# SBUF laid out so that every tile read by TensorE begins at a multiple of 512 bytes, with the kernel's small tiles together at the beginning

## The chip, the core and the metric

The kernel runs on one core of one Trainium2 chip. The metric is the device time of one execution in microseconds (us); three executions of the kernel before took 1311.05, 1311.29 and 1311.66 us, so the median is 1311.29 us.

## The reference, cut to what matters

The program is a two-layer decoder trunk over one sequence of 512 tokens, 1024 wide, in float32. In short form:

```python
h = x
h = h + rglru_mixer(rmsnorm(h), ...)   # layer 0: w_in 1024 x 2560, conv, gates, scan, w_out 1280 x 1024
h = h + conv_ffn(rmsnorm(h), ...)      # w_in 1024 x 6144, conv of width 3, gelu(a) * b, w_out 3072 x 1024
h = h + nsa_mixer(rmsnorm(h), ...)     # layer 1: q, k, v; compressed, selected and window attention, gates, w_out
h = h + conv_ffn(rmsnorm(h), ...)
return rmsnorm(h)
```

Nearly all of the arithmetic is in the weight matrices: two feed-forward blocks, the recurrent block's projections and the attention block's projections. The result has to be close to float32.

## The kernel before, in words

**Products.** Activations are kept transposed: a tile of 128 features (partitions) by 512 tokens. Every float32 operand is split into a high part that TensorE's one-pass float32 form holds exactly (`hi`) and the rest (`lo`), and a product is three matmuls, `hi*hi`, `hi*lo` and `lo*hi`, accumulated in one PSUM bank. This is `mm3` (lines 211 to 217): line 213 multiplies the weights' high part with the activations' high part, line 214 the same weights with the activations' low part, line 215 the weights' low part with the activations' high part. The weights are the stationary operand (128 x 128, that is 512 bytes of each partition), the activations the moving operand (128 x 512, 2048 bytes of each partition).

**Weights.** A weight tile is 128 x 1024 (4096 bytes of each partition), eight stationary operands. `_dma` loads it as `wraw` through SP's queue, `_split` makes `whi` on ScalarE (line 184) and `wlo` on VectorE or GpSimd (line 185). `wtile` (line 151) gives two weight tiles of three a buffer in the pool `wp` (named `wraw`, `whi`, `wlo`) and every third one a buffer in the pool `wx` (named `wrawx`, `whix`, `wlox`); during the attention block `wx` is closed and all tiles come from `wp`.

**Activations.** The normalised inputs of a block are `xh0` to `xh7` and `xl0` to `xl7`; the hidden values of a feed-forward block are `fh0` to `fh23` and `fl0` to `fl23` (`ffn`, from line 630); those of the recurrent block `hh`, `hl`, its gates' inputs `ch`, `cl` with weights `ghi`, `glo`; the attention block has keys `K2h`, `K2l`, queries `qa`, `qb`, values `V2`, probabilities `P`, `ph`, `sq`, outputs `oh`, `ol` (for two of the four groups these reuse the names `K2h`, `K2l`).

**Order of the work.** The four blocks follow one another: recurrent, feed-forward, attention, feed-forward. In the first, second and fourth the order of the instructions is the program's; in the attention block every step has a due time (`FILL`, `WIN`, `LAT_S`, `LAT_V` and so on), and the steps are issued sorted by it (`at` and `perform`), each engine in that order. In that block projections and output products stand between the attention's own matmuls.

**Where tiles lie.** The places in SBUF follow from the program alone: pools stand one behind another, tiles in a pool stand in the order in which their names first appear, and each is rounded up to 32 bytes of a partition. The program's own scratch and constants take the first 16,512 bytes, which is 128 more than a multiple of 512. Counted modulo 512, the kernel before places things so. First come `prm` (1520 bytes, rounded to 1536) and `cst` (3176, rounded to 3200), so `x0` to `x7` begin at 256. `mhalf` and `warm` take 64 bytes, so `xh`, `xl` and the pool `wp` (`wraw`, `whi`, `wlo`) begin at 320, and so do `ssum` and `sq`. `nv` and `rtok` (64 bytes) put `rbc` at 384, and the two `fv` and two `frt` (128 bytes) bring the next pool to 0: `wx` (`wrawx`, `whix`, `wlox`), and behind it `fh` and `fl`, or the attention's `K2h`, `K2l`, `V2`. In the recurrent block nine tiles of 64 bytes and `sp` (96) stand before `hh` and `hl`, which begin at 160, as do `ghi`, `glo`, `ch` and `cl`. In the attention block `gtok` (768 bytes) puts `qa` and `qb` at 256, the eight tiles `sm`, `nm`, `c` (256 bytes) put `P` at 0, `mx` (64) puts `ph` at 64, and `smc` (64) puts `ch`, `cl`, `oh`, `ol` at 128.

Of the kernel before, what the change touches and what calls it, by code (L numbers as in the profile page):

```python
# [10 lines left out]
F32 = mybir.dt.float32  # L11
F32R = mybir.dt.float32r
AF = mybir.ActivationFunctionType
# [6 lines left out]
NB = 10  # L20
# [51 lines left out]
P_CW, P_CB, P_GB, P_AP = 40, 80, 90, 110  # L72
P_FW, P_FB = 120, 264
P_B1, P_POS = 312, 316
P_END = 380

C_ID, C_D, C_DC, C_SC, C_ROW, C_ONE, C_SL = 0, 128, 640, 768, 776, 777, 778
C_END = 794
# [22 lines left out]
class Trunk:  # L101
# [166 lines left out]
    def norm_finish(self, newps):  # L268
        T, V = self.T, self.V
        ps = newps()  # L270
        for t in range(4):
            T.matmul(ps[:, t:t + 1], self.ssum[:, 128 * t:128 * t + 128], self.cst[:, C_ONE:C_ONE + 1],
                     start=True, stop=True)
        v = self.np_.tile([128, 4], F32, name="nv", bufs=1)
        V.tensor_scalar(v, ps[:, :4], 1.0 / 1024.0, 1e-6, op0=ALU.mult, op1=ALU.add)
        self.rtok = self.np_.tile([128, 4], F32, name="rtok", bufs=1)
        self.G.tensor_tensor(self.rtok, v, self.mhalf, op=ALU.pow)

    def norm_spread(self, newps):
# [5 lines left out]
        self.rbc = self.np_.tile([128, NT], F32, name="rbc", bufs=1)  # L285
        self.S.activation(self.rbc, ps, AF.Copy)


    def start(self):
        nc, a = self.nc, self.a  # L290
        self.prm = self.cp.tile([128, P_END], F32, name="prm")
        self.cst = self.cp.tile([128, C_END], F32, name="cst")
        self.x = [self.cp.tile([128, NT], F32, name=f"x{k}") for k in range(KD)]
        self.plan()
        self.tins, self.tgrp, self.manual = [], None, False
        self.mhalf = self.cp.tile([128, 4], F32, name="mhalf")
        self.V.memset(self.mhalf, -0.5)
        warm = self.cp.tile([128, 4], F32, name="warm")
        self.S.activation(warm, self.mhalf, AF.Copy)
        self._dma(0)  # L300
        self._dma(1)
        self.wd = 2
        nc.scalar.dma_start(self.prm[:, :P_CW], a["prm"][:, :P_CW])
        self._half(0, 0, True)
        for k in range(KD):
            nc.sync.dma_start(self.x[k], a["x"][k])
            if k in START:
                self._half(*START[k], True)
        self._dma(2)
        self.wd = 3  # L310
        nc.sync.dma_start(self.cst, a["cst"])
        nc.sync.dma_start(self.prm[:, P_CW:], a["prm"][:, P_CW:])
        self.ident = self.cst[:, C_ID:C_ID + 128]

    def warm_up(self, n):
# [53 lines left out]
    def final(self, ts, newps, sq=None):  # L369


        T, V, prm = self.T, self.V, self.prm
        n = (ts.stop - ts.start) // 128
        parts = [self.ssum[:, ts]] + ([sq] if sq is not None else [])
        ps = newps()
        for t in range(n):
            for j, p in enumerate(parts):
                T.matmul(ps[:, t:t + 1], p[:, 128 * t:128 * t + 128], self.cst[:, C_ONE:C_ONE + 1],
                         start=(j == 0), stop=(j == len(parts) - 1))
        v = self.np_.tile([128, 4], F32, name="fv")  # L380
        V.tensor_scalar(v[:, :n], ps[:, :n], 1.0 / 1024.0, 1e-6, op0=ALU.mult, op1=ALU.add)
        rt = self.np_.tile([128, 4], F32, name="frt")
        self.G.tensor_tensor(rt[:, :n], v[:, :n], self.mhalf[:, :n], op=ALU.pow)
        yield
        ps = newps()
# [219 lines left out]
    def softplus(self, hp):  # L605
        V, S = self.V, self.S
        t = lambda nm: hp.tile([128, NB], F32, name="sp_" + nm)
# [13 lines left out]
            V.tensor_scalar(po, po, 2.0 / k, None, op0=ALU.add)  # L621
        V.tensor_mul(po, po, q)
        V.tensor_add(po, po, mx)
        sp = hp.tile([128, 2, NB], F32, name="sp")
        V.tensor_scalar(sp[:, 0], po, 4.0, None, op0=ALU.mult)
        V.tensor_scalar(sp[:, 1], po, -8.0, None, op0=ALU.mult)
        return sp
# [72 lines left out]
    def nsa(self):  # L700
        S, V, G, T, prm, cst = self.S, self.V, self.G, self.T, self.prm, self.cst
        tc, a = self.tc, self.a
        with ExitStack() as s:
# [6 lines left out]

            Vc = kp.tile([128, 4, 4, 128], F32R, name="Vc")
            G.memset(Vc.bitcast(F32), 0.0)
            gtok = kp.tile([128, 4, 48], F32, name="gtok")
            Q = {}

            def project():
# [182 lines left out]
                S.activation(Vc[rs, i, :, :64], pkv[rs], AF.Copy)  # L899
                V.tensor_sub(Vc[rs, i, :, 64:], pkv[rs], Vc[rs, i, :, :64].bitcast(F32))  # L900

            junk = self.np_.tile([128, 4], F32, name="nv", bufs=1)
            self.tact(junk, self.mhalf, AF.Exp)
            q_tile(1)
            cs.close()
# [19 lines left out]
            def compressed(g, s0, d, newps=None):  # L925
# [25 lines left out]
                    V.tensor_add(v4(st["X"]), v4(st["pc"]), dt.unsqueeze(2).to_broadcast([128, 4, 4, 32]))  # L951

                def mx():
                    st["mx"] = ap_.tile([128, 16], F32, name="mx", bufs=1)
                    V.reduce_max(st["mx"], v3(st["X"]), axis=AX.X)

                def sub():
# [5 lines left out]
                        self.G.tensor_mul(v4(st["X"])[:, i], v4(st["X"])[:, i], sl)  # L963

                def norm():
                    sm = st["sm"] = ap_.tile([128, 4, 4], F32, name="smc", bufs=1)
                    V.reduce_sum(sm.rearrange("p i r -> p (i r)"), v3(st["X"]), axis=AX.X)
                    V.reciprocal(sm, sm)
                    V.tensor_mul(sm, sm, gtok[:, :, 4 * g:4 * g + 4])
# [38 lines left out]
            def scores(g, i, brs, steps):  # L1008
# [20 lines left out]

                def red(b):  # L1030
                    if b == 0:
                        st["sm"] = ap_.tile([128, 2, 4], F32, name="sm", bufs=3)
                        st["nm"] = ap_.tile([128, 2, 4], F32, name="nm")
                        st["c"] = ap_.tile([128, 2, 4], F32, name="c", bufs=3)
                    pt = newP(F32)
                    for r in range(b * per, b * per + per):
                        for br in brs:
                            sl = cols(r, br)
                            Ps[g, i, br].append(pt[:, sl])
                            V.tensor_tensor_reduce(pt[:, sl], st["sp", b][:, sl],  # L1040
                                                   cst[:, C_D + 384 - 128 * i:C_D + 512], -SLOPE[4 * g + r],
                                                   3e38, ALU.add, ALU.min, accum_out=st["nm"][:, br, r:r + 1])
# [246 lines left out]
```

## Time and profile before

| | |
|---|---|
| median of three executions | 1311.29 us |
| the profiled execution | 1311.32 us |
| its span, first to last instruction | 1309.5 us |
| granted TensorE clock, mean of the span | 0.996 |
| PE busy (matmul) | 1295.0 us, 99% |
| PE weight loads | 1062.5 us, 81% |
| VectorE, ScalarE, GpSimd busy | 787.2, 612.8, 242.2 us |
| matmuls | 6158 |

A matmul's recorded end is modelled and lies past the start of the next one, so a matmul of 512 columns is shown with about 390 ns while the next one starts about 227 ns after it. How long a matmul holds the engine is therefore read from starts: the start of one row of the timeline, the start of a later one, and the count of matmuls between. Where two groups of the same shape have different means, the difference of the means is the difference of the distances between starts.

### The profile page before, as it was taken

To read this page: it belongs to the slowest core of one execution; us is meant where nothing else is said; L and a number is where in the kernel's file an instruction comes from. 1 tells how busy PE (TensorE), PEld (TensorE's weight loads), DVE (VectorE), ACT (ScalarE), POOL (GpSimd) and SP (SyncE) were. 2 spreads that over 40 slices of the span, in tenths; PEclk is the share of its full clock that TensorE was granted. 3 is DMA by queue.
4 is the path that set the end of the run, shared out by engine and by line. 5 is a ranking of instruction groups with operands and counts; after the bars stand their busy time and mean duration, and the time that the engine had idled before them with its cause. 6 is when DMAs were issued, how large, how long until landed. Compare 5 with 4: busy or idle time off the path is not lost.

```text
span 1309.5 us, 16269 instructions
## 1 busy us (share of the span) xinstructions
PE 1295.0 (99%) x6158; PEld 1062.5 (81%) x6158; DVE 787.2 (60%) x1270; ACT 612.8 (47%) x983; POOL 242.2 (18%) x254
## 2 busy tenths in 40 slices
PE   9999999999999999999999999999999999999996
PEld 7888888888888888888787778888888888888886
DVE  7899875555555533327557978875655555542222
ACT  6788743333333322222458878865433333332220
POOL 0222440000000001115017667633000000000110
PEclk9999999999999999999999999999999999999998
DMA  7232232232232222223311010113222232222221
GB/s 243 89 100 85 90 97 97 97 97 97 97 97 97 96 98 97 90 101 121 121 66 33 33 33 33 34 33 129 97 97 97 97 97 97 97 97 96 89 73 65
DMA packets 36222, 117.71 MB, mean 90 GB/s; under 512 B 4144, under 2 KB 7728, under 8 KB 36144
## 3 DMA queue, kind: packets, MB, share of 16 engines
q1 hardware_dynamic: 34848, 115.61, 26.5%
q8 instruction: 48, 0.79, 0.3%
q10 hardware_dynamic: 1296, 1.07, 0.2%
q14 instruction: 30, 0.25, 0.1%
HBM read 114.57 MB, written 2.10 MB: 89 GB/s over the span
## 4 chain that ended last, share of the span: by engine, by line
PE 94%; DVE 2%; ACT 1%; issue 1%; POOL 1%; DMA 0%; SPq 0%; POOLq 0%; DVEq 0%; ACTq 0%
PE bank L213 28%; PE bank L214 28%; PE bank L215 27%; PE bank L1081 2%; PE bank L1101 1%; PE bank L1097 1%; PE bank L873 1%; PE bank L1027 1%; PE bank L1028 1%; PE bank L832 1%; PE bank L831 1%; PE bank L833 1%; DVE P L1040 0%; PE bank L1100 0%; ACT P L228 0%
## 5 line engine op out<-in xcount | busy, mean ns | idle before, releaser
L213 PE MATMUL bank<-xh,whi 128*128 128x512 f32 x760 | 297.8, 392 | 0.5 <-DVE qn L754 0.2
L215 PE MATMUL bank<-xh,wlo 128*128 128x512 f32 x760 | 296.2, 390 | 0.5 <-DVE wlo L185 0.5
L214 PE MATMUL bank<-xl,whi 128*128 128x512 f32 x760 | 296.2, 390 | 0.3 <-DVE xl L256 0.3
L184 ACT ACTIVATE whi<-wraw 128x1024 fp32r<-128x1024 f32 x143 | 151.3, 1058 | 303.8 <-PE bank L214 251.1
L185 DVE TENSOR_TENSOR wlo<-wraw,whi 128x1024 fp32r<-128x1024 f32 x133 | 163.5, 1230 | 127.4 <-ACT whi L184 117.0
L266 POOL TENSOR_TENSOR ssum<-ssum,sq 128x512 f32<-128x512 f32 x27 | 44.8, 1658 | 766.3 <-issue 581.1
L213 PEld LDWEIGHTS bank<-xh,whi 128*128 128x128 f32 x760 | 142.8, 188 | 32.5 <-DVE nm L1040 0.8
L215 PEld LDWEIGHTS bank<-xh,wlo 128*128 128x128 f32 x760 | 142.6, 188 | 31.0 <-DVE wlo L185 1.0
L214 PEld LDWEIGHTS bank<-xl,whi 128*128 128x128 f32 x760 | 142.8, 188 | 29.6 <-DVE xl L256 0.8
L184 ACT ACTIVATE whix<-wrawx 128x1024 fp32r<-128x1024 f32 x57 | 60.4, 1060 | 131.0 <-PE bank L214 129.6
L214 PE MATMUL bank<-xl,whix 128*128 128x512 f32 x296 | 116.5, 394 | 0.0
L213 PE MATMUL bank<-xh,whix 128*128 128x512 f32 x296 | 116.1, 392 | 0.0
L215 PE MATMUL bank<-xh,wlox 128*128 128x512 f32 x296 | 115.1, 389 | 0.0
L213 PE MATMUL bank<-fh,whi 128*128 128x512 f32 (+1 forms) x272 | 104.0, 382 | 0.0
L214 PE MATMUL bank<-fl,whi 128*128 128x512 f32 (+1 forms) x272 | 103.9, 382 | 0.0
L215 PE MATMUL bank<-fh,wlo 128*128 128x512 f32 (+1 forms) x272 | 103.9, 382 | 0.0
L1057 POOL TENSOR_SCALAR P<-P,c,gtok 128x512 f32<-128x512 f32 (+3 forms) x128 | 79.4, 634 | 99.9 <-DVE c L1053 85.2
L185 DVE TENSOR_TENSOR wlox<-wrawx,whix 128x1024 fp32r<-128x1024 f32 x57 | 70.8, 1242 | 40.9 <-ACT whix L184 40.8
L648 DVE TENSOR_TENSOR ar<-bank,rbc 128x512 f32<-128x512 f32 x48 | 33.2, 691 | 99.6 <-PE bank L215 99.6
L658 DVE TENSOR_TENSOR b<-bank,rbc 128x512 f32<-128x512 f32 x48 | 33.2, 691 | 86.2 <-PE bank L215 86.2
L228 ACT ACTIVATE P<-P,nm 128x512 f32<-128x512 f32 (+3 forms) x128 | 70.9, 556 | 16.9 <-DVE nm L1040 13.8
L228 ACT ACTIVATE t<-t 128x512 f32<-128x512 f32 x48 | 30.4, 632 | 98.0 <-DVE t L654 98.0
(219 smaller groups left out, 2311.5 us busy)
## 6 DMA issues: line engine op xcount, KB each, us to landing
wraw<-in_ffn_in_dram SPq DMA_DIRECT2D x65, 512.0 KB, 3.3
wraw<-in_ffn_out_dram SPq DMA_DIRECT2D x32, 512.0 KB, 3.3
wrawx<-in_ffn_in_dram SPq DMA_DIRECT2D x31, 512.0 KB, 3.3
wrawx<-in_ffn_out_dram SPq DMA_DIRECT2D x16, 512.0 KB, 3.2
wraw<-in_nsa_in_dram SPq DMA_DIRECT2D x16, 512.0 KB, 3.3
wraw<-in_lru_in_dram SPq DMA_DIRECT2D x12, 512.0 KB, 3.7
w<-in_cmp_w_dram SPq DMA_DIRECT2D x8, 512.0 KB, 4.5
wraw<-in_nsa_out_dram SPq DMA_DIRECT2D x8, 512.0 KB, 3.3
```

What stands on the lines that cost most here:

```text
L184: self.S.activation(hi[:, c], raw[:, c], AF.Copy)
L185: (eng or (self.G if self.manual and WLO else self.V)).tensor_sub(lo[:, c], raw[:, c], hi[:, c].bitcast(F32))
L213: ins = mm(ps, wh, xh, start=first, stop=False)
L214: mm(ps, wh, xl, start=False, stop=False)
L215: end = mm(ps, wl, xh, start=False, stop=last)
L228: ins = self.S.activation(out, in_, func, **k)
L266: self.sq_eng.tensor_add(self.ssum, self.ssum, sq)
L648: V.tensor_mul(ar, pa, self.rbc)
L658: V.tensor_mul(b, pb, self.rbc)
L831: T.matmul(pv[t], xh[:, ts], hi[:, sl], start=(k == 0), stop=False)
L1057: G.tensor_scalar(Ps[g, i, br][r], Ps[g, i, br][r], st["c"][:, br, r:r + 1], gtok[:, i, gc:gc + 1], op0=ALU.mult, op1=ALU.mult)
L1081: T.transpose(st["t", kt][:, 128 * r:128 * r + 128], Ps[u][r][:, 128 * kt:128 * kt + 128], self.ident)
```

## The change

Every small tile (`sm`, `nm`, `c`, `mx`, `fv`, `mhalf`, `gtok`, `nv`, `rtok`, `frt`) becomes a permanent tile at the beginning of SBUF. Tiles that came in turn from a pool (`sm`, `nm`, `c`, `fv`, `frt`) are now lists, and `next` hands them out in rotation with as many buffers as before. `smc` shares the tile of `mx`; `warm` and the first `fv` share that of `nv`. `prm` is made four columns longer and `sp` wider, which only pads.

The sizes add up as follows. From 128: eight tiles of 32, `mx` with 64, `fv` and `mhalf` with 32 each make 384, so `cst` begins at 0. `cst` with 3200, `gtok` with 768 and `nv`, `rtok` and two `frt` with 128 make 4096, so `prm` begins at 0, and with 1536 bytes it leaves `x0` at 0. From there on all tiles are multiples of 512 bytes: `xh`, `xl`, `wp`, `wx`, `fh`, `fl`, `K2h`, `K2l`, `V2`, `qa`, `qb`, `P`, `ph`, `oh`, `ol` begin at 0. In the recurrent block nine tiles of 64 and `sp` with 448 make 1024, so `hh`, `hl`, `ch`, `cl`, `ghi`, `glo` begin at 0 as well. Of the tiles that TensorE reads, the second of the two `G` (7936 bytes) alone begins at 256.

```diff
     def norm_finish(self, newps):
...
-        v = self.np_.tile([128, 4], F32, name="nv", bufs=1)
+        v = self.nv
         V.tensor_scalar(v, ps[:, :4], 1.0 / 1024.0, 1e-6, op0=ALU.mult, op1=ALU.add)
-        self.rtok = self.np_.tile([128, 4], F32, name="rtok", bufs=1)
         self.G.tensor_tensor(self.rtok, v, self.mhalf, op=ALU.pow)
+    def next(self, name):
+        t = self.few[name]
+        t.append(t.pop(0))
+        return t[-1]
     def start(self):
-        self.prm = self.cp.tile([128, P_END], F32, name="prm")
-        self.cst = self.cp.tile([128, C_END], F32, name="cst")
+        one = lambda name, shape: self.cp.tile([128] + shape, F32, name=name)
+        few = lambda name, shape, n: [one(f"{name}{j}", shape) for j in range(n)]
+        self.few = {"sm": few("sm", [2, 4], 3), "nm": few("nm", [2, 4], 2), "c": few("c", [2, 4], 3),
+                    "mx": few("mx", [16], 1)}
+        fv, self.mhalf = one("fv", [4]), one("mhalf", [4])
+        self.cst = one("cst", [C_END])
+        self.gtok = one("gtok", [4, 48])
+        self.nv, self.rtok = one("nv", [4]), one("rtok", [4])
+        self.few["fv"], self.few["frt"] = [self.nv, fv], few("frt", [4], 2)
+        self.prm = one("prm", [P_END + 4])
...
-        self.mhalf = self.cp.tile([128, 4], F32, name="mhalf")
         self.V.memset(self.mhalf, -0.5)
-        warm = self.cp.tile([128, 4], F32, name="warm")
-        self.S.activation(warm, self.mhalf, AF.Copy)
+        self.S.activation(self.nv, self.mhalf, AF.Copy)
...
-        nc.sync.dma_start(self.prm[:, P_CW:], a["prm"][:, P_CW:])
+        nc.sync.dma_start(self.prm[:, P_CW:P_END], a["prm"][:, P_CW:])
     def final(self, ts, newps, sq=None):
-        v = self.np_.tile([128, 4], F32, name="fv")
+        v = self.next("fv")
...
-        rt = self.np_.tile([128, 4], F32, name="frt")
+        rt = self.next("frt")
     def softplus(self, hp):
-        sp = hp.tile([128, 2, NB], F32, name="sp")
+        sp = hp.tile([128, 112], F32, name="sp")[:, :2 * NB].rearrange("p (a n) -> p a n", a=2)
     def nsa(self):
-            gtok = kp.tile([128, 4, 48], F32, name="gtok")
+            gtok = self.gtok
...
-            junk = self.np_.tile([128, 4], F32, name="nv", bufs=1)
+            junk = self.nv
...
-                    st["mx"] = ap_.tile([128, 16], F32, name="mx", bufs=1)
+                    st["mx"] = self.next("mx")
...
-                    sm = st["sm"] = ap_.tile([128, 4, 4], F32, name="smc", bufs=1)
+                    sm = st["sm"] = st["mx"].rearrange("p (i r) -> p i r", i=4)
...
-                        st["sm"] = ap_.tile([128, 2, 4], F32, name="sm", bufs=3)
-                        st["nm"] = ap_.tile([128, 2, 4], F32, name="nm")
-                        st["c"] = ap_.tile([128, 2, 4], F32, name="c", bufs=3)
+                        st["sm"] = self.next("sm")
+                        st["nm"] = self.next("nm")
+                        st["c"] = self.next("c")
```

## Rows read from the trace of the kernel before

**Rows 1.** From the page: busy time of the engines with shares of the span and instruction counts, the granted TensorE clock in 40 slices, and the chain that ended last by engine.
```profile
PE 1295.0 (99%) x6158; PEld 1062.5 (81%) x6158; DVE 787.2 (60%) x1270; ACT 612.8 (47%) x983; POOL 242.2 (18%) x254
...
PEclk9999999999999999999999999999999999999998
...
PE 94%; DVE 2%; ACT 1%; issue 1%; POOL 1%; DMA 0%; SPq 0%; POOLq 0%; DVEq 0%; ACTq 0%
```

**Rows 2.** The waits of PE, longest first: us in total, times, longest.
```profile
PE bank L321 <- DVE mhalf L297: 1.4, 1, 1.4
PE bank L378 <- ACT sq L684: 1.3, 1, 1.3
```

**Rows 3.** Groups by line and form, PE alone, 452.2 to 585 us (the first feed-forward block's output products): count | busy us, mean ns of one | idle before.
```profile
L213 PE MATMUL bank<-fh,whi 128*128 128x512 f32 x128 | 50.6, 395 | 0.0
L214 PE MATMUL bank<-fl,whi 128*128 128x512 f32 x128 | 50.6, 395 | 0.0
...
L214 PE MATMUL bank<-fl,whix 128*128 128x512 f32 x64 | 25.0, 390 | 0.0
L213 PE MATMUL bank<-fh,whix 128*128 128x512 f32 x64 | 24.9, 390 | 0.0
```

**Rows 4.** The same view, 201 to 452 us (the first feed-forward block's input products).
```profile
L213 PE MATMUL bank<-xh,whi 128*128 128x512 f32 x240 | 93.4, 389 | 0.0
...
L214 PE MATMUL bank<-xl,whix 128*128 128x512 f32 x128 | 50.4, 394 | 0.0
L213 PE MATMUL bank<-xh,whix 128*128 128x512 f32 x128 | 50.2, 393 | 0.0
L215 PE MATMUL bank<-xh,wlox 128*128 128x512 f32 x128 | 49.7, 389 | 0.0
```

**Rows 5.** The timeline of PE in the output products: start us, us, engine, line. Between the first and the second row stand 48 matmuls (two weight tiles in `wp`), between the second and the last 24 (one in `wx`), 6 of them before the third row.
```profile
468.77 0.40 PE L213 MATMUL bank<-fh,whi 128*128 128x512 f32 x1
...
479.97 0.39 PE L213 MATMUL bank<-fh,whix 128*128 128x512 f32 x1
...
481.36 0.39 PE L213 MATMUL bank<-fh,whix 128*128 128x512 f32 x1
...
485.44 0.40 PE L213 MATMUL bank<-fh,whi 128*128 128x512 f32 x1
```

**Rows 6.** The timeline of PE in the input products: 21 matmuls from the first to the second row, 48 from the second to the third.
```profile
299.93 0.39 PE L213 MATMUL bank<-xh,whix 128*128 128x512 f32 x1
...
304.74 0.39 PE L213 MATMUL bank<-xh,whi 128*128 128x512 f32 x1
...
315.62 0.39 PE L213 MATMUL bank<-xh,whix 128*128 128x512 f32 x1
```

**Rows 7.** The timeline of PE in the recurrent block's output products: 24 matmuls from each row to the next.
```profile
160.16 0.39 PE L213 MATMUL bank<-hh,whi 128*128 128x512 f32 x1
...
165.76 0.39 PE L213 MATMUL bank<-hh,whix 128*128 128x512 f32 x1
...
171.38 0.40 PE L213 MATMUL bank<-hh,whi 128*128 128x512 f32 x1
```

**Rows 8.** Groups by line and form, PE alone, 50 to 128 us (the recurrent block's gates, between its input products).
```profile
L214 PE MATMUL bank<-cl,ghi 128*128 128x512 f32 x12 | 4.7, 395 | 0.0
L215 PE MATMUL bank<-ch,glo 128*128 128x512 f32 x12 | 4.7, 395 | 0.0
```

**Rows 9.** Groups by line and form, PE alone, 700 to 895 us (the attention block's timed part).
```profile
L1097 PE MATMUL bank<-ph,V 128*128 128x512 f32 x76 | 31.5, 415 | 0.0
...
L215 PE MATMUL bank<-xh,wlo 128*128 128x512 f32 x48 | 18.9, 394 | 0.0
...
L215 PE MATMUL bank<-oh,wlo 128*128 128x512 f32 x32 | 12.6, 394 | 0.0
...
L214 PE MATMUL bank<-K2l,whi 128*128 128x512 f32 x28 | 11.0, 394 | 0.0
```

**Rows 10.** Busy time by stretch in the attention block: the stretch, its length, then busy us and (count) of each engine, granted clock, DMA share, GB/s.
```profile
700.00:750.00 50.00, 48.97 (x268) 38.75 (x266) 43.35 (x126) 41.67 (x105) 32.19 (x42) 1.00 0.09 33
750.00:800.00 50.00, 49.81 (x301) 40.15 (x300) 39.72 (x121) 40.96 (x105) 36.82 (x46) 1.00 0.10 32
800.00:850.00 50.00, 50.00 (x338) 41.05 (x338) 42.02 (x131) 41.91 (x110) 32.98 (x45) 1.00 0.09 30
850.00:895.00 45.00, 45.00 (x228) 36.83 (x228) 35.26 (x79) 30.52 (x64) 17.63 (x21) 1.00 0.15 50
```

**Rows 11.** The timeline of PE in the last column of the last block, where a matmul has 256 columns: 24 matmuls from each row to the next.
```profile
1278.61 0.28 PE L213 MATMUL bank<-fh,whi 128*128 128x256 f32 x1
...
1281.43 0.28 PE L213 MATMUL bank<-fh,whix 128*128 128x256 f32 x1
...
1284.31 0.28 PE L213 MATMUL bank<-fh,whi 128*128 128x256 f32 x1
```

**Rows 12.** From the page: the same subtraction on VectorE with tiles in `wp` and in `wx`, and ScalarE's exponentials of the attention block, which read `nm` and add up into `sm`.
```profile
L185 DVE TENSOR_TENSOR wlo<-wraw,whi 128x1024 fp32r<-128x1024 f32 x133 | 163.5, 1230 | 127.4 <-ACT whi L184 117.0
...
L185 DVE TENSOR_TENSOR wlox<-wrawx,whix 128x1024 fp32r<-128x1024 f32 x57 | 70.8, 1242 | 40.9 <-ACT whix L184 40.8
...
L228 ACT ACTIVATE P<-P,nm 128x512 f32<-128x512 f32 (+3 forms) x128 | 70.9, 556 | 16.9 <-DVE nm L1040 13.8
```

## The prediction, made before the result was known

> **What bounds the kernel now.** I read the page first: PE is busy for 99% of the span at the full granted clock, 2.4 GHz, and the chain of work that ended last is 94% PE [rows 1]. Then PE's waits: the longest are 1.4 and 1.3 us, once each [rows 2]. So from start to end TensorE issues one matmul behind the other, and the kernel's time is the number of matmuls times the distance between their starts. No other engine, no queue and no DMA has to get faster for the time to fall; a change of some nanoseconds in that distance is multiplied by some 5,100 matmuls of 512 columns (6158 in all [rows 1], under a thousand of them shorter).
>
> Is that distance one constant? The groups say no. In the output products of the first feed-forward block the same moving tiles `fh`, `fl` meet weights in `wp` with a mean of 395 ns and weights in `wx` with 390 [rows 3]. In its input products the order is turned round: `xh` with `wp` 389, `xh` and `xl` with `wx` 393 and 394, only the line with `wlox` at 389 [rows 4]. The means hold a modelled end, so I take the distances from starts:
> - `fh`, `fl` (at 0 modulo 512) with `wp` (at 320): 48 matmuls in 479.97 - 468.77 = 11.20 us, 233.3 ns each [rows 5].
> - the same with `wx` (at 0): 24 in 5.47 us, 227.9 each; the first six take 1.39 us, 231.7 each, and the other 18 take 4.08 us, 226.7 each [rows 5].
> - `xh`, `xl` (at 320) with `wp` (at 320): 48 in 10.88 us, 226.7 each; with `wx` (at 0): 21 in 4.81 us, 229.0 each [rows 6].
> - `hh`, `hl` (at 160) with `wp` or `wx`: 24 in 5.60 and 5.62 us, 233.3 and 234.2 each [rows 7].
>
> Neither buffer is slow by itself: `wp` is at 226.7 with `xh` and at 233.3 with `fh`, `wx` at 229.0 with `xh` and 226.7 with `fh`. What counts is the pair. Where moving and stationary tile begin at the same place modulo 512 the distance settles at 226.7 ns, at 320 as well as at 0; where they differ it is 229.0 to 234.2. A stationary operand is one of eight in its tile, 512 bytes apart, and both fast rows run through all eight, so multiples above 512 make no difference that can be seen there.
>
> **The change part by part.** After it all these tiles begin at 0 modulo 512, and so do their operands, since `xh` and the hidden tiles are read from their beginning and weights in steps of 512. Each stage then goes to 226.7 ns.
> - Input products of the two feed-forward blocks: 2 x 48 tiles x 24 = 2304 matmuls, a third with `wx`. 768 x (229.0 - 226.7) = 1.8 us. The other two thirds are at 226.7 already.
> - Output products: eight columns of 72 in the first block, seven in the second, 1080 matmuls. 720 with `wp`: x (233.3 - 226.7) = 4.8 us. 360 with `wx`: x (227.9 - 226.7) = 0.4 us, since the six slow ones are what is left of the pair before.
> - Recurrent block, output products: 8 x 30 = 240 matmuls x (233.7 - 226.7) = 1.7 us.
> - Recurrent block, input products and gates: six of the 20 tiles lie in `wx`, 144 x 2.3 = 0.3 us; 60 gate matmuls at 395 [rows 8] against 389 [rows 4], 0.4 us. Together 0.7 us.
> - Last column: 144 matmuls of 256 columns, where the pair counts the other way: 24 with `wp` in 2.82 us (117.5 each), 24 with `wx` in 2.88 (120.0) [rows 11]. 96 change from the first to the second: a loss of 0.2 us.
> - Attention block, timed part. `xh`, `oh` and `K2l` against weights stand at 394 [rows 9] where the settled pair has 389 [rows 4]. Three lines each of 48, 32 and 28, and twice 76 matmuls with `V2` make some 476; x 5 ns = 2.4 us. The upper bound adds the 415 of `ph` with `V2` as if all of it came from the pair: 76 x 21 ns more, 1.6 us, so 4.0 us. The lower bound is nothing: between 700 and 750 us VectorE is busy for 43.35 of 50 us and ScalarE for 41.67, and PE already has a microsecond idle [rows 10]; there a quicker PE only waits. From 800 to 895 us PE is busy throughout [rows 10] and the gain stays. I take two thirds of 2.4, 1.6 us.
> - Other short matmuls (transposes, scores, products of the compression): no row has them in two layouts. The nearest, rows 11, differ by 2.5 ns; for under a thousand that is 2.4 us at most either way. I take nothing, as no sign is known.
> - VectorE, ScalarE and GpSimd read and write at other places. The one operation that stands in both layouts is 1230 ns in `wp` and 1242 in `wx` [rows 12], 1%; if all 133 took that, 133 x 12 ns = 1.6 us of VectorE's time, hidden under PE outside the attention block.
> - Small tiles. `sm`, `nm`, `c`, `fv` and `frt` keep their number of buffers, so each write waits for the same earlier reads as before. `smc` in `mx`'s tile means that the next group's maximum waits for GpSimd's scaling of this group, as its sum did; the compressed parts are due some 20 us apart. `warm` in `nv` waits for nothing that isn't long done. No DMA is added or moved past another, and no wait is put on PE. I count nothing; if a unit's reductions did have to wait for one exponential of the unit ahead, 0.56 us [rows 12], 28 units would cost 15.6 us.
>
> Sum: 1.8 + 4.8 + 0.4 + 1.7 + 0.7 - 0.2 + 1.6 = 10.8 us. The sum is made against the profiled execution, 1311.32 us for a span of 1309.5, so 1.8 us lie around the span and do not change; it stands 0.03 us above the median of 1311.29. Forecast: 1311.3 - 10.8 = 1300.5 us.
>
> The Trainium skill speaks against such a gain. "TensorE: Matmul & The Clock Gate", section "Step-by-step: what each phase is for", says that PE has two independent read ports, one for the moving operand and one for weight loads, so that loading the next weights takes no read bandwidth from the running matmul. By it the place of the weights could not matter, and the time would stay at 1311.3 us. This trace disagrees: the moving tiles of rows 3 are the same and only the weights' place differs.
>
> **The rivals.**
> - The place is not the cause (no change, 1311.3 us): the two reads do not disturb each other, and the pairs differ in something that the new layout keeps, say the order of the buffers or the engines' writes beside them. For it: only four kinds of pair are shown. Against: one and the same buffer is fast in one pair and slow in the other, and 240 matmuls of a group have one mean. I give it 5%.
> - The slow rhythm stays (slower, about 1322.5 us): an aligned pair has a slow rhythm too, the six matmuls of 231.7 ns at the begin of each `wx` tile [rows 5], and if the stream falls into it after an interruption and remains there, every stage runs at 231.7. Input products: 1536 x 5.0 + 768 x 2.7 = 9.8 us more; output products with `wp` 720 x 1.6 = 1.2 less, with `wx` 360 x 3.8 = 1.4 more; recurrent inputs 336 x 5.0 = 1.7 more, outputs 240 x 2.0 = 0.5 less: 11.2 us more. It decides from about two fifths on: 5,100 x 5.0 ns x 0.42 eats the 10.8 us. Against: the slow stretch ends after six, and 48 behind a `wx` tile go at 226.7 [rows 6]. 4%.
> - The attention block's small tiles make its engines wait (slower, 1300.5 + 15.6 = 1316 us): each unit's reduction waits for an exponential. For it: VectorE and ScalarE are nearly full there [rows 10], so a wait is not absorbed; it turns the sign from 0.4 us for each of 28 units on. Against: the buffers' number is unchanged. 3%.
>
> **How the numbers follow.** The forecast has 88%. Its own spread: the attention block between 0 and 4.0 us gives 1302.1 to 1298.1, short matmuls 2.4 us either way. If the settled rate is reached only as in a whole `wx` tile, 227.9 for all 5,100, 1.2 ns x 5,100 = 6.1 us of the gain are lost: 1306.6. So the range is 1296.5 to 1306.5 us; the other cases lie outside it. A measurement of this kernel can tell a difference of about 0.2%, 2.6 us, from none, so faster means under 1308.7 us. All of the forecast's spread lies there, so faster has 0.88; the first rival makes the 0.05 of the same, the two others the 0.07 of slower.
>
> **What would show it.** Right: in the profile after, the groups `fh` with `whi`, `hh` with either and `xh` with `whix` all have the mean of `xh` with `whi` now, 389 to 390, and two weight tiles of the output products take 10.88 us in place of 11.20; the granted clock and PE's share stay. The attention's step: the length from its first exponential to the last output product falls by 1 to 3 us. The last column gets slower, 2.88 us for each of its tiles. Wrong: groups that keep their 395 (first rival), 393 to 394 for all (second), or waits of PE on `nm`, `sm` or `P` in the attention block (third).

## The result and the profile after

The changed kernel takes 1301.33 us, the median of five executions (1299.36 to 1301.59); five of the kernel before gave 1311.29. The ratio is 0.9921, with a 95% interval from 0.9908 to 0.9935: 10 us less, 0.8%, clear of noise. The forecast was 1300.5 us, with a range from 1296.5 to 1306.5. The profiled execution took 1301.59 us, its span 1299.8.

From the page after, the lines that answer to [rows 1]:

```profile
PE 1285.6 (99%) x6158; PEld 1062.6 (82%) x6158; DVE 787.4 (61%) x1270; ACT 612.4 (47%) x983; POOL 241.5 (19%) x254
...
PE 94%; DVE 2%; ACT 1%; issue 1%; POOL 1%; DMA 1%; SPq 0%; POOLq 0%; DVEq 0%; ACTq 0%
```

The counts of instructions, the busy times of the other engines and the shape of the chain are the same to within a microsecond or a percent. Only PE's busy time fell, by 9.4 us. Nothing was taken out of the program; its matmuls stand closer together.

Groups of PE by line and form after, 450 to 580 us (the first feed-forward block's output products; count | busy us, mean ns of one | idle before), to be held against [rows 3]:

```profile
L213 PE MATMUL bank<-fh,whi 128*128 128x512 f32 x128 | 49.8, 389 | 0.0
L214 PE MATMUL bank<-fl,whi 128*128 128x512 f32 x128 | 49.8, 389 | 0.0
L213 PE MATMUL bank<-fh,whix 128*128 128x512 f32 x64 | 24.9, 389 | 0.0
```

The same view after, 199.6 to 449.8 us (its input products), to be held against [rows 4]:

```profile
L213 PE MATMUL bank<-xh,whi 128*128 128x512 f32 x240 | 93.5, 389 | 0.0
...
L213 PE MATMUL bank<-xh,whix 128*128 128x512 f32 x128 | 49.9, 390 | 0.0
...
L214 PE MATMUL bank<-xl,whix 128*128 128x512 f32 x128 | 49.8, 389 | 0.0
```

All are at 389 or 390. The timeline of PE in the output products after (start us, us; 48 matmuls from the first row to the second, 24 to the third), against [rows 5]:

```profile
466.21 0.39 PE L213 MATMUL bank<-fh,whi 128*128 128x512 f32 x1
...
477.09 0.39 PE L213 MATMUL bank<-fh,whix 128*128 128x512 f32 x1
...
482.53 0.39 PE L213 MATMUL bank<-fh,whi 128*128 128x512 f32 x1
```

10.88 us for 48, where it was 11.20, and 5.44 for 24, where it was 5.47: 226.7 ns each. The slow first six behind a change of buffer are gone as well.

Stage by stage, each from the start of its first matmul to the start of the next stage's first, read from the timelines of three profiles. The third column is a run of the experiments below, the same layout moved by 256 bytes:

| stage, us | before | after | after, moved | forecast change |
|---|---|---|---|---|
| up to the first product | 5.87 | 5.57 | 5.87 | 0 |
| recurrent block, inputs and gates | 124.89 | 124.90 | 123.82 | -0.7 |
| recurrent block, outputs | 57.45 | 56.15 | 56.19 | -1.7 |
| first feed-forward block, inputs | 263.89 | 263.27 | 263.27 | -0.9 |
| first feed-forward block, outputs | 133.34 | 130.56 | 130.56 | -2.8 |
| attention, from projections to first score | 90.67 | 91.64 | 90.73 | 0 |
| attention, first to last score | 188.63 | 188.29 | 188.31 | -1.6 with the next |
| attention, last output products | 33.39 | 32.85 | 32.84 | |
| second feed-forward block, inputs | 263.82 | 263.00 | 263.00 | -0.9 |
| second feed-forward block, outputs | 134.93 | 132.71 | 132.71 | -2.2 |
| from the last product to the end | 12.65 | 10.86 | 10.66 | 0 |

Three of these differences come from DMAs and not from the pairs of tiles. Two rows among PE's waits after have none before them:

```profile
PE bank L213 <- ACT xh L255: 0.8, 1, 0.8
PE bank L886 <- DMA w<-in_cmp_w_dram: 0.7, 1, 0.7
```

The first is the load of `x` at the start that landed later, the second a weight load of the compression. Against the moved layout, whose profile has neither wait, the two stages are 1.1 and 0.9 us longer. The first stands in no other profile. The second may belong to the quicker stream: a wait of 0.2 to 1.1 us for the same load stands in seven of the ten other profiles with tiles moved, and in neither of the two with the old places (the kernel before and its lightened form below). In the lightened new layout it is the longest:

```profile
PE bank L886 <- DMA w<-in_cmp_w_dram: 1.1, 1, 1.1
```

The tail is the other way round. The rows on the output's DMAs (KB each, us from issue to landing) in the profile before and in that after:

```profile
out_dram<-x SPq DMA_DIRECT2D x4, 128.0 KB, 2.4
```

```profile
out_dram<-x SPq DMA_DIRECT2D x4, 128.0 KB, 1.7
```

The old layout with an edit in the attention block, below, landed them in 1.7 us too and ended 10.70 us after the start of its last product. So the old layout does not by itself have the slow tail of the profile before, and the 1.8 us gained there are not counted as the layout's.

### The profile page after: what moved, and what is told of

Its sections match the earlier page's. It is cut to its first block, busy times and chain, and to the rows that moved or that the text cites. A ratio compares the mean times of both kernels' runs of the same rounds, so it can differ in the third digit from the quotient of the medians.

```text
span 1299.8 us, 16266 instructions
## 1 busy us (share of the span) xinstructions
PE 1285.6 (99%) x6158; PEld 1062.6 (82%) x6158; DVE 787.4 (61%) x1270; ACT 612.4 (47%) x983; POOL 241.5 (19%) x254
## 4 chain that ended last, share of the span: by engine, by line
PE 94%; DVE 2%; ACT 1%; issue 1%; POOL 1%; DMA 1%; SPq 0%; POOLq 0%; DVEq 0%; ACTq 0%
PE bank L213 28%; PE bank L214 28%; PE bank L215 27%; PE bank L1094 2%; PE bank L1114 1%; PE bank L1110 1%; PE bank L1040 1%; PE bank L1041 1%; PE bank L886 1%; PE bank L845 1%; PE bank L844 1%; PE bank L846 1%; DVE P L1053 0%; PE bank L1113 0%; DMA w<-in_cmp_w_dram 0%
```

## The experiments

The runs of the sweeps, of `wlo` and of the lightened kernels were executed once each, the others four or five times. Two theories stood against each other: that only the distance between the moving and the stationary tile counts, and that multiples of 512 bytes themselves, or the small tiles at the beginning, do.

**The whole layout moved by 256 bytes.**

```diff
+        one("pad", [64])
         self.few = {"sm": few("sm", [2, 4], 3), "nm": few("nm", [2, 4], 2), "c": few("c", [2, 4], 3),
```

> The new layout with 256 bytes put ahead of cst, so that every tile read by TensorE begins at 256 modulo 512. Theory (only the distance between moving and stationary tile modulo 512 counts): all pairs keep distance 0, so the groups fh with whi, hh with whi and xh with whix stay at 389 to 390 ns, 24 matmuls of the output products take 5.44 us (226.7 ns each), and the time is that of the new layout, 1299 to 1302 us. Rival (the multiple of 512 itself counts): these groups go to 393 to 397 ns and the time to 1308 us or more.

Measured: 1299.39 us (1298.92 to 1299.85), against 1309.95 for the kernel before on the same chip, a ratio of 0.9915 (0.9901 to 0.9929). `fh` and `fl` with `whi` and with `whix` have 389 ns throughout, and every undisturbed stage has the length of the new layout to 0.05 us (table above). No tile that TensorE reads begins at a multiple of 512 there, apart from the second `G`. The multiple of 512 is not the cause.

**One pad of 64 bytes in the kernel before.** If the distance is all, the old layout needs only its later pools moved to where `xh` and `wp` stand.

```diff
         rt = self.np_.tile([128, 4], F32, name="frt")
+        if ts.start == 0:
+            self.np_.tile([128, 16], F32, name="pad", bufs=1)
```

> The kernel before with one unused tile of 64 bytes at the end of the pool np, so that wx, fh, K2h, V2, P begin at 64 modulo 256, as xh and wp (320) do already; the small tiles stay where they were and nothing begins at a multiple of 512. hh moves to 224. Theory (distance of the pair modulo 256): the feed-forward blocks run as in the new layout, input products 263.0 to 263.3 us (before 263.9 and 263.8) and output products 130.6 and 132.7 us (before 133.3 and 134.9); the recurrent output products stay at 57.5 us (distance 160); together 6.5 to 7 us under the kernel before. Rival (multiples of 512, or the permanent small tiles, bring the gain): these stages stay at the values of before and so does the time.

Measured: 1302.99 us against 1310.6 on the same chip, 0.9944 (0.9932 to 0.9957), 7.6 us less, where 6.5 to 7 were expected. Output products 130.56 and 132.71 us, input products 263.04 and 263.00: the new layout's values, 6.7 us less than before in these four stages. The groups of PE in the first block's output products (451 to 581 us) and in the recurrent block's (144 to 187 us):

```profile
L213 PE MATMUL bank<-fh,whi 128*128 128x512 f32 x127 | 49.4, 389 | 0.0
...
L213 PE MATMUL bank<-fh,whix 128*128 128x512 f32 x64 | 24.9, 389 | 0.0
```

```profile
L213 PE MATMUL bank<-hh,whi 128*128 128x512 f32 x36 | 14.3, 396 | 0.0
...
L213 PE MATMUL bank<-hh,whix 128*128 128x512 f32 x26 | 10.3, 396 | 0.0
```

`fh` is quick, `hh`, whose distance is 160, is not, and its stage keeps 57.60 us. The small tiles keep their pools and their order, so making them permanent is not the cause either.

**The distance, step by step.** The hidden tiles of the feed-forward blocks were put at other places, six pairs `fh`, `fl` at each, with all weights at 0. The second run has the distances 288 to 512 in place of 32 to 256.

```diff
+                if f % 6 == 0:
+                    o = (0,) + OFFS[l]
+                    hp.tile([128, (o[f // 6 + 1] - o[f // 6]) // 4], F32, name=f"pad{f}")
                 hh = hp.tile([128, NT], F32R, name=f"fh{f}")
```

> The new layout with pads among the hidden tiles of the feed-forward blocks, so that groups of six pairs fh, fl begin at 32, 64, 96, 128 (first block) and 160, 192, 224, 256 (second block) modulo 512 while the weights stay at 0. Theory (the distance moving minus stationary alone): 160 gives 234.2 ns and 192 gives 233.3 ns from start to start once settled, as before the change with the weights at 0 and 320 and the activations at 160 and 0; the other distances lie between 226.7 and 236 and none is below 226.7. Rival (places themselves count): 160 and 192 give other values than these by more than 1 ns. The time rises by 576 x 5 to 576 x 7 ns in the first block and as much in the second, to some 1306 to 1309 us.

> As the run before, with 288, 320, 352, 384 in the first block and 416, 448, 480, 512 in the second. Theory (distance alone): 320 gives 229.0, 352 gives 233.3 and 512 gives 226.7 ns once settled; others between 226.7 and 236. Rival (places themselves): 320 and 352 give other values by more than 1 ns, or 512 is not 226.7. Time 1304 to 1309 us.

A third run cut the tiles out of larger ones, for distances under 32:

```diff
+                if f % 6 == 0:
+                    big = hp.tile([128, 12 * NT + 64], F32R, name=f"big{f}")
+                c = OFFS[l][f // 6] // 4 + 2 * NT * (f % 6)
+                hh, hl = big[:, c:c + NT], big[:, c + NT:c + 2 * NT]
-                hh = hp.tile([128, NT], F32R, name=f"fh{f}")
-                hl = hp.tile([128, NT], F32R, name=f"fl{f}")
```

> The new layout with the hidden tiles of the feed-forward blocks cut out of larger tiles, so that groups of six pairs begin 4, 8, 12, 16 bytes (first block) and 20, 24, 28, 48 bytes (second block) past a multiple of 256, the weights at 0. Theory A (only a whole multiple of 256 is quick): every one of these distances settles at 229 to 236 ns. Theory B (the reads are in pieces of some bytes, and a shift within one piece costs nothing): the small ones, 4 to 12 bytes at least, settle at 226.7. None is under 226 in either.

They took 1305.3, 1305.93 and 1306.8 us; the first is a little under the 1306 to 1309 expected of it. The timeline of PE in one column of the first run (line 214 is 213 of the others); from each row to the next 18 matmuls, at distances 32, 64, 96 and 128:

```profile
465.57 0.39 PE L214 MATMUL bank<-fh,whi 128*128 128x512 f32 x1
...
469.77 0.39 PE L214 MATMUL bank<-fh,whi 128*128 128x512 f32 x1
...
473.89 0.40 PE L214 MATMUL bank<-fh,whi 128*128 128x512 f32 x1
...
478.10 0.40 PE L214 MATMUL bank<-fh,whix 128*128 128x512 f32 x1
...
482.30 0.39 PE L214 MATMUL bank<-fh,whi 128*128 128x512 f32 x1
```

4.20, 4.12, 4.21 and 4.20 us, that is 233, 229, 234 and 233 ns each. Over all columns, the mean distance between starts in ns:

| moving minus stationary, bytes | 32 | 64 | 96 | 128 | 160 | 192 | 224 | 256 |
|---|---|---|---|---|---|---|---|---|
| first run | 233.2 | 228.8 | 233.9 | 233.3 | 233.8 | 232.7 | 232.8 | 227.0 |
| second run, 256 bytes more | 233.2 | 228.8 | 233.9 | 233.3 | 233.8 | 232.7 | 232.8 | 227.0 |

| moving minus stationary modulo 256, bytes | 4 | 8 | 12 | 16 | 20 | 24 | 28 | 48 |
|---|---|---|---|---|---|---|---|---|
| third run | 237.3 | 232.1 | 228.9 | 231.8 | 237.7 | 235.0 | 229.1 | 233.3 |

The two runs agree to a tenth at every distance, so the period is 256 bytes, not 512. Once settled (from the ninth of a group on), 160, 192, 320 and 352 give 234.0, 233.3, 229.2 and 233.1, as forecast from the old layout, where other tiles at other places had those distances; 256 and 512 give 226.7. In the third run no distance is quick: shifts of 4 and 20 bytes cost the most, some 11 ns. Theory A holds in that only a whole multiple of 256 is quick; its span of 229 to 236 ns was too narrow, with settled values from 228.8 (28 bytes) to 239.3 (20 bytes).

**Which weights.** Here `wlo` alone stands 32 bytes off.

```diff
+            self.wp.tile([128, 8], F32, name="pad1", bufs=1)
             t = self.wtile(i, F32R, "wlo")
+            self.wp.tile([128, 56], F32, name="pad2", bufs=1)
```

> The new layout with the tiles wlo in wp alone moved 32 bytes, so that of the three matmuls of a product the third (line 215) has its own weights at distance 224 from its activations, and the second (line 214) has the next weights at that distance; wlox stays. Theory N (the weights being loaded for the next matmul count): from the start of line 214 to that of 215 it is 230 ns or more, and the two others stay at 226 to 228. Theory C (the weights in use count): from the start of line 215 to the next start it is 230 ns or more, and the two others stay. Either way the mean of the three in whi tiles is 228 to 230 ns, and 226.7 in whix tiles.

The groups of PE, 201 to 452 us (lines 223, 224, 225 are 213, 214, 215 of the others):

```profile
L224 PE MATMUL bank<-xl,whi 128*128 128x512 f32 x240 | 96.0, 400 | 0.0
L223 PE MATMUL bank<-xh,whi 128*128 128x512 f32 x240 | 94.7, 395 | 0.0
L225 PE MATMUL bank<-xh,wlo 128*128 128x512 f32 x240 | 93.4, 389 | 0.0
```

The matmul whose own weights are off keeps 389. The one before it, during which those weights are loaded, rises to 400. So the tile that a moving tile must match is the one being loaded beside it, and theory C falls. But the first line rises too, to 395, though both its own and its next weights are at 0: theory N is not the whole of it, and the mean over the three is 395 - 162 = 233 ns, above the 228 to 230 expected (389 stands for 227, so a mean stands some 162 over the distance). Measured from starts, lines 223, 224 and 225 have 232.6, 238.8 and 228.0 ns. The run takes 1319.94 us, 9 us more than the kernel before on the same chip and some 19 more than the new layout: `wlo` in the wrong place costs about twice what the whole change brought.

**Two parts taken back.**

```diff
-        sp = hp.tile([128, 112], F32, name="sp")[:, :2 * NB].rearrange("p (a n) -> p a n", a=2)
+        sp = hp.tile([128, 2, NB], F32, name="sp")
...
+                    if not pads:
+                        pads.append(ap_.tile([128, 16], F32, name="pad1", bufs=1))
                     st["h", kt] = ap_.tile([128, NT], F32R, name="ph", bufs=3)
+                    if len(pads) == 1:
+                        pads.append(ap_.tile([128, 16], F32, name="pad2", bufs=1))
```

> The new layout with two parts taken back: in the recurrent block hh, hl, ch, cl, ghi, glo begin at 160 again, and in the attention block ph begins at 64 and ch, cl, oh, ol at 128 again; the feed-forward blocks keep the new layout. Theory: the recurrent block's output products take 24 matmuls in 5.6 us again (1.7 us in all) and the gates 395 ns (0.4 us); the attention block's timed part, which gained 0.8 us by the change and not the 1.6 us forecast, stays within 0.5 us of the new layout because PE waits there for VectorE, ScalarE and GpSimd and because short runs of matmuls do not settle; together 2 to 2.5 us above the new layout. Rival: the attention block's gain came from these tiles, and its timed part gets 0.8 us or more longer, together 3 us or more.

Measured: 1301.38 us (1301.31 to 1302.3), 2.0 us above the moved layout's 1299.39 on the same chip. The recurrent outputs are back at 57.60 us (1.4 more), its inputs and gates at 124.34 (0.5 more); the attention block's two stages are at 188.45 and 32.88, 0.2 more together. The recurrent block's gain in the outputs is the layout's. The attention block hardly minds where these tiles are. In the last output products the gain stayed although `oh` and `ol` stood elsewhere (32.88 us; 33.39 before): there 120 matmuls in a row have `K2h` and `K2l` as activations, which kept the new places.

**Why the attention block gains so little.** It gained 0.9 us where 1.6 were forecast, on the ground that a quicker PE would wait there for the other engines. The rival reason is that its matmuls, although aligned now, are not quick. Groups of PE after, 700 to 890 us, against [rows 9]:

```profile
L1110 PE MATMUL bank<-ph,V 128*128 128x512 f32 x73 | 30.2, 413 | 0.0
...
L215 PE MATMUL bank<-xh,wlo 128*128 128x512 f32 x47 | 18.5, 393 | 0.0
...
L215 PE MATMUL bank<-oh,wlo 128*128 128x512 f32 x32 | 12.6, 393 | 0.0
```

393, one less than before and four more than 389. First the projections were issued in sixes.

```diff
-                    for k in range(KD):
-                        at(steps[k], "T", lambda k=k: ch(k))
+                    for k in range(0, KD, 2):
+                        at(steps[k], "T", lambda k=k: (ch(k), ch(k + 1)))
```

> The new layout; in the attention block's timed part the projections and output products are issued six matmuls at a time at half as many due times, where they were issued three at a time. Theory S (short runs do not settle at 226.7 because the rhythm needs about six matmuls): the groups oh with whi and xh with whi there fall from 230 to 233 ns towards 228, and the stretch from the first score to the last gets 0.5 to 1.5 us shorter than 188.3 us. Theory W (PE waits for VectorE, ScalarE and GpSimd): the groups may fall, but the stretch stays at 188.3 us or gets longer.

Measured: 1305.16 us, slower than the new layout; first to last score 191.70 us in place of 188.3. The groups stay:

```profile
L215 PE MATMUL bank<-xh,wlo 128*128 128x512 f32 x46 | 18.1, 393 | 0.0
...
L215 PE MATMUL bank<-oh,wlo 128*128 128x512 f32 x32 | 12.6, 392 | 0.0
```

This looked like theory W, but it decides little: the due times no longer fit, and six is near the length at which an old pair settled. So the other engines were relieved instead, in both layouts, by leaving out two of their steps.

```diff
-                            at(s1 + LAT_S[3], "G", lambda r=r, br=br: sc(r, br))
+                            pass
...
-                    st["l", kt] = self.np_.tile([128, NT], F32R, name="sq")
-                    V.tensor_sub(st["l", kt], st["t", kt], st["h", kt].bitcast(F32))
+                    st["l", kt] = st["h", kt]
```

> The layout of the kernel before, with two steps of the attention block left out: GpSimd's scaling of the probabilities P by the reciprocal sum and the gate, and VectorE's subtraction that makes the low part of the transposed probabilities (the second product takes the high part once more). TensorE's instructions are the same in number and shape. It stands beside the same edit in the new layout. From the first score to the last it was 188.6 us in the kernel before. Theory W (PE waits there for VectorE, ScalarE and GpSimd): 187.5 us or less here. Theory R (PE is not held up; matmuls in a mixed stream do not settle): 188.3 to 188.9.

> The same two steps left out in the new layout. With all steps the new layout gained 0.3 us from the first score to the last (188.6 to 188.3) and 0.5 us from there to the second feed-forward block. Theory W: with the other engines relieved the layout's gain comes through, 1.2 us or more between this run and the same edit in the old layout. Theory R: the gain stays under 0.6 us, since pairs at distance 0 there still take 230 to 233 ns from start to start.

Measured: 1303.72 us in the old layout and 1295.84 in the new on the same chip; first to last score 183.68 and 183.28 us; the last output products 33.38 and 32.86. Busy times in that stretch (stretch, length, then busy us and count of PE, PE's weight loads, VectorE, ScalarE, GpSimd, granted clock, DMA share, GB/s), new layout with all steps, then new layout relieved:

```profile
672.10:860.40 188.30, 186.40 (x1138) 150.49 (x1137) 157.00 (x475) 155.19 (x397) 125.03 (x164) 1.00 0.10 32
```

```profile
671.40:854.60 183.20, 183.13 (x1137) 150.90 (x1136) 112.90 (x402) 152.84 (x396) 48.53 (x42) 1.00 0.10 33
```

PE did wait for the other engines, as theory W had it of the old layout (187.5 us or less) and theory R had not (188.3 or more): relieved, the stretch is 5 us shorter and PE has no idle left. Of these 5 us 1.8 had stood as idle time, 3.3 within PE's busy time. But the layout's gain does not come through: it is 0.4 us between the scores and 0.5 behind them, 0.9 together, as with all steps (0.3 and 0.5), where theory W asked for 1.2 or more. On the gain, then, theory R was right. The last run looks at its ground directly: a whole projection of 24 matmuls in a row.

```diff
-                    for k in range(KD):
-                        at(steps[k], "T", lambda k=k: ch(k))
+                    at(steps[0], "T", lambda: [ch(k) for k in range(KD)])
```

> The lightened kernel in the new layout (GpSimd's scaling and VectorE's low part of the probabilities left out), with each projection of the attention block's timed part issued as 24 matmuls in a row and each output product as 12, where they were cut into threes. Theory R (an aligned pair needs an undisturbed run to settle): by place in the run the distance between starts is 229 ns or more up to about the sixth and 226 to 227.5 from about the tenth on. Rival (something else in the attention block, such as the other engines' work beside it, keeps pairs slow): 229 ns or more at every place. Nothing is expected of the time, since the due times no longer fit.

It took 1310.2 us, as its steps no longer fit their due times. The timeline of PE in one projection; nine matmuls from the first row to the second, three to the third, twelve to the fourth:

```profile
699.68 0.40 PE L213 MATMUL bank<-xh,whi 128*128 128x512 f32 x1
...
701.77 0.39 PE L213 MATMUL bank<-xh,whi 128*128 128x512 f32 x1
...
702.45 0.39 PE L213 MATMUL bank<-xh,whi 128*128 128x512 f32 x1
...
705.17 0.39 PE L1109 MATMUL bank<-ph,V 128*128 128x512 f32 x1
```

2.09 us for nine, 232 ns each; then 0.68 for three and 2.72 for twelve, 226.7 each. By place in the run, the mean over the runs of 12 and 24 is 231 to 234 from the second to the fourth matmul, 229 from the fifth to the seventh, 228 from the eighth to the tenth, and 226.7 after that, but for a run's last matmul, beside which another kind of pair is loaded. So the rival falls: beside the work that is left to the other engines here, a pair does get quick. An aligned pair needs some six to ten undisturbed matmuls to settle; in threes and sixes between transposes and scores it does not get there. The same is seen elsewhere: the timeline of PE after, behind a stop at the beginning of the first feed-forward block, nine matmuls from the first row to the second and three to the third:

```profile
193.47 0.39 PE L214 MATMUL bank<-xl,whi 128*128 128x512 f32 x1
...
195.55 0.39 PE L214 MATMUL bank<-xl,whi 128*128 128x512 f32 x1
...
196.23 0.39 PE L214 MATMUL bank<-xl,whi 128*128 128x512 f32 x1
```

2.08 us for nine, 231 ns each, then 0.68 for three.

## Why the prediction was right, point by point

- **What bounds the kernel, and the pair as the cause.** Right, and shown from both sides: the pad of 64 bytes gives the feed-forward blocks' gain and the moved layout the whole of it with the tiles away from multiples of 512, and the steps of the distance give the old layout's values at new places. The Trainium skill's statement, in "TensorE: Matmul & The Clock Gate", section "Step-by-step: what each phase is for", that weight loads take no read bandwidth from a running matmul, does not fit these float32 operands: 226.7 to 239 ns by the place of a tile alone. That the two reads disturb each other is an inference; the runs show only that the place of the tile being loaded sets the running matmul's pace.
- **Modulo 512.** Too coarse. The prediction said "begin at the same place modulo 512", which is what the old layout could show; the runs show 256.
- **Feed-forward blocks.** Inputs: forecast 1.8 us, measured 0.62 + 0.82 = 1.4. Outputs: forecast 5.2 less 0.2 for the last column, measured 2.78 + 2.22 = 5.0 us. The last column does get slower, 2.87 and 2.88 us for two of its tiles, where [rows 11] have 2.82 and 2.88. The timeline of PE after, 24 matmuls from each row to the next:

```profile
1270.47 0.28 PE L213 MATMUL bank<-fh,whi 128*128 128x256 f32 x1
...
1273.34 0.28 PE L213 MATMUL bank<-fh,whix 128*128 128x256 f32 x1
...
1276.22 0.28 PE L213 MATMUL bank<-fh,whi 128*128 128x256 f32 x1
```

- **Recurrent block.** Forecast 1.7 and 0.7, measured 1.3 and, without the late load, 1.1 us: 2.4 together, as forecast, but by two misses that cancel. In the outputs the pace fell as forecast, from 233.6 to 227.0 ns; 0.35 us went back because the first matmuls behind the gates now stand apart, five from the first row to the second in 1.49 us where five took 1.17 before (the profile names no wait for it):

```profile
144.07 0.39 PE L213 MATMUL bank<-hh,whix 128*128 128x512 f32 x1
...
145.56 0.39 PE L215 MATMUL bank<-hh,wlox 128*128 128x512 f32 x1
```

  The 1.1 us of the inputs hold the luck of the loads at the start: the output products began at 129.97 and 130.76 us in the two profiles of the old places, and at 129.3 to 129.7 in seven of the new layout. The price of the gates, 0.4 us, measured 0.2 (their first line, which rows 8 leave out, had 392), and its cause was not named: `ch` and `ghi` were at the same place before (160), so by the rule as stated they should have been quick. PE's timeline in the first gate, six matmuls from row to row, before and after:

```profile
36.09 0.40 PE L213 MATMUL bank<-ch,ghi 128*128 128x512 f32 x1
...
37.48 0.39 PE L213 MATMUL bank<-xh,whix 128*128 128x512 f32 x1
```

```profile
36.55 0.39 PE L213 MATMUL bank<-ch,ghi 128*128 128x512 f32 x1
...
37.91 0.39 PE L213 MATMUL bank<-xh,whix 128*128 128x512 f32 x1
```

  231.7 and 226.7 ns each, and after the change eight of the ten gates have 226.7 or 226.8. So it is not that six matmuls are too few: before, the stream came to the gates from tiles at 320, and at each change of place the pair had to settle anew; after, all stand at one place and the stream goes through. With the gates put back to 160 and the stream left at 0, in the run with two parts taken back, the first nine take some 230 ns each again.
- **Attention block.** The step that failed. "There a quicker PE only waits" is not why the gain stays away; with the waits gone it is no larger. What keeps it away is that runs of three and six between other matmuls do not settle. The term was mis-sized at 1.6 us and measured 0.9, of which 0.5 lie behind the last score; the 1 to 3 us named as its sign did not come.
- **Small tiles, other engines, short matmuls.** Counted at nothing, and nothing is seen: the busy times agree, the transposes of `P` have a mean of 272 ns in both profiles, and PE's waits for `nm` and `P` are 0.4 us each, where they were 0.3 and 0.4. "No wait is put on PE" did not hold for the compression's weights (0.7 us in the profile after); whether the quicker stream causes that wait was not tested.
- **The sum.** 10.8 us forecast; the moved layout's column shows 9.6 from the first product to the last. Of the missing 1.2 us, 0.7 are the attention block's and 0.4 the feed-forward inputs'. The slow rhythm does exist in an aligned pair, as the second rival had it, but it ends after some six to ten matmuls and so costs only where runs are short. That the medians differ by 10.0 us, so near to the forecast, is in part luck: in the profile after, the two late loads (2.0 us) and the quicker tail (1.8 us) cancel.

## What to carry to other kernels

When matmuls stand back to back with a new stationary tile each, compare the distance between their starts by pair of tiles; groups of one shape with different means point to where the tiles lie. For float32 tiles with 128 stationary and 512 moving columns, lay out every pair so that moving and next stationary operand begin at the same place modulo 256 bytes: a pad of 64 bytes brought three quarters of this gain. The full gain needs a stream of more than ten such matmuls between stops. A change to other tiles at the same place was no stop (the gates, in sixes, at 226.7 ns); a change to tiles at another place was. With 256 moving columns an equal place was slower, 120 ns against 117.5 at 192 modulo 256.

## What the runs showed of the hardware that was not expected

- The distance between starts depends on the two tiles' distance modulo 256 bytes in an irregular way: 226.7 ns at 0, 228.8 to 229.2 at 12, 28 and 64, 237 to 239 at 4 and 20, 231 to 235 at the others.
- It is a rhythm with a memory. After a stop an aligned pair runs at some 231 ns for five to nine matmuls and then stays at 226.7. Behind pairs 192 apart it took six [rows 5]; behind pairs 64 apart it was at 226.7 at once [rows 6]. At other distances a pattern can repeat: long parts of `hh` before have 231, 232 and 237 ns in turn.
- What counts is the operand being loaded for the next matmul, not the one in use; but moving `wlo` alone also slowed the second matmul behind that one, to 232.6 ns. Why was not found.
- No distance, in steps of 32 bytes and at eight finer ones, is quicker than 226.7 ns.
